# Differential attention: scores on two 64-row halves of the array in three products, and one joint maximum for each softmax component

## The chip, the core and the metric

The program runs on one core of a Trainium2 chip. Five engines work side by side, each through its own queue in order: TensorE (PE in the profile, its weight loads PEld), VectorE (DVE), ScalarE (ACT), GpSimd (POOL), and SyncE (SP), which here only issues transfers. The metric is the device time of one execution in microseconds (us), less is better; a time of before is the median of three runs.

## The reference

Two layers; each normalises x (2048 rows of 1024), projects it, feeds three head groups, joins them through an output projection and adds the result to x. The change touches the middle group alone, differential attention with 4 heads, each with two score components of 64 dimensions:

```python
q = rope(q, pos) * (DIFF_HD ** -0.5)      # (2, B, 4 heads, L, 64)
k = rope(k, pos)
def block(qblk):                          # 128 queries
    s = jnp.einsum('cbhqd,cbhkd->cbhqk', qblk, k).astype(jnp.float32)
    p = jax.nn.softmax(s, axis=-1)
    w = p[0] - lam * p[1]
    return jnp.einsum('bhqk,bhkv->bhqv', w.astype(v.dtype), v)
o = lax.map(block, qb)
o = rms_norm(o, norm_w) * (1.0 - lambda_init)
```

The other two groups are gated linear recurrences; the part of them that reads their carried states (`Inter` below) is computed in the same stage of the kernel as the attention.

## The kernel before, in words

Each layer runs through a projection stage (with the scans of the recurrences), the attention stage, and the output projection. In the attention stage a `Unit` is 128 queries of one head, so a layer has 64 units and the program 128. Products keep fp32 accuracy by a split in a high and a low part: q is split in `aqh` and `aql` (by POOL, L723 and L725, for 256 queries at once), k in its two parts when it is made. The 128 partitions of `ks` hold the 64 dimensions of k's high part and the 64 of its low part, those of q hold the 64 dimensions twice; one 128-row matmul of `aqh` with `ks` therefore gives two products, that of `aql` two more (L866, L867).

A unit passes through four *steps*, one for each score tile of 128 queries by 1024 keys: steps 0 and 1 are the first and second half of the keys for component 0, steps 2 and 3 those for component 1. PE's step is: `scores` (four matmuls of 512 columns into a score tile `s` of two banks), `values` (`po`, the weights times v, for an earlier unit), `transposes` (`pt`, of an earlier unit's weights). DVE takes each tile's maximum (`mx`, L871); ACT takes the exponentials (`e`, L880) out of the tile, and with that frees it; DVE forms e0 + factor * e1 (`combine`, L909); PE transposes that, ACT copies the transposed weights to SBUF (`wt`, L919), PE multiplies them with v.

For component 0 both exponentials wait for the maximum over both tiles (L874, then `exps` in step 2). For component 1 each tile is taken with its own maximum as soon as that is there (step 3 for the tile of step 2, step 0 of the next unit for the tile of step 3); `lows`, `weights`, `total` and `factors` bring the two halves to one scale afterwards.

The order within every engine's queue is written by hand: `tc.manual_schedule` keeps the order of the `at_lag` calls, where lag is the number of steps after the unit's first one. Score tiles come from `two_banks`: three buffers in rotation, so that a tile is written when the third tile before it has been read. `Inter`, one for every second unit from unit 16 to 46 (16 in a layer), takes one turn of this rotation as well: its 12 matmuls `poi` (L816) are issued ahead of the scores of step 3, and ACT's `fetch` (L821) frees it in the step after.

```python
def two_banks(name):
    turn[0] += 1
    key, bufs = (("b", 2), ("b", 2), ("t", 1))[turn[0] % 3]
    return psum[key][1].tile([P, 2, 512], F32, tag="two", name=name, bufs=bufs)
```

The transposed tiles `pt` have one buffer beside that of `po`. POOL has q's split, the multiplication of the result by the gate, the state updates at the stage's start (L768, L771), Inter's sums, and the split of the output weights near the stage's end (`load_wo`, units 50 to 57).

Of the kernel before, what the change touches and what calls it, by code (L numbers as in the profile page):

```python
# [16 lines left out]
ALU = mybir.AluOpType  # L17
# [43 lines left out]
def tile_hybrid_encoder(  # L61
# [178 lines left out]
    for l in range(DEPTH):  # L240
# [15 lines left out]
        with ExitStack() as s1:  # L256
# [67 lines left out]
            def do_qk(c0, cb, which, part):  # L324
                hc = slice(4 * cb, 4 * cb + 4)
                w = wload(c0 + 256 * cb, 256, part, halves=True)
                for g in (2 * part, 2 * part + 1):
# [5 lines left out]
                    for half, (a, b, op) in enumerate(((p1, p2, ALU.subtract), (p2, p1, ALU.add))):  # L333
# [382 lines left out]
            def load_q(h, qp):  # L716
                qr = ak.tile([P, 2, 256], F32, tag="aq", name="aq", bufs=2)
                for half in range(2):
                    for s in range(2):
                        p0 = 64 * half + 32 * s  # L720
# [27 lines left out]
        with ExitStack() as s2:  # L748
# [93 lines left out]
            class Unit:  # L842
                """One block of 128 queries of one head; s counts its tiles of scores (component, half of the keys)."""

                def __init__(self, i):
# [8 lines left out]
                    self.sm = at.tile([P, 4], F32, tag="sm", name="sm", bufs=4)  # L854
                    self.gm = at.tile([P, 10], F32, tag="gam", name="gam", bufs=4)
# [13 lines left out]
                def maxima(self, k):  # L869
                    mx = self.mx  # L870
                    nc.vector.tensor_reduce(mx[:, k:k + 1], self.s[k].rearrange("p a n -> p (a n)"), axis=AX.X, op=ALU.max,  # L871
                                            negate=True)
# [10 lines left out]
                def lows(self):  # L883
                    nc.vector.tensor_tensor(self.mx[:, 5:6], self.mx[:, 2:3], self.mx[:, 3:4], op=ALU.min)

                def sums(self):
                    gm, sm = self.gm, self.sm
                    nc.vector.tensor_tensor(gm[:, 2:3], sm[:, 0:1], sm[:, 1:2], op=ALU.add)

                def sums2(self):  # L890
                    gm = self.gm
                    nc.vector.tensor_scalar(gm[:, 1:2], gm[:, 2:3], neglam, None, op0=ALU.mult)
# [228 lines left out]
```

## Time and profile before

| | us |
|---|---|
| runs | 3752.49, 3755.73, 3758.89; median 3755.73 |
| span of the profiled execution, first to last instruction | 3752.0 |
| mean granted TensorE clock over the span | 0.982 of full speed |
| busy: PE | 3534.9 (94%) |
| busy: DVE | 2691.2 (72%) |
| busy: ACT | 2203.1 (59%) |
| busy: POOL | 1868.5 (50%) |

The profile has no time of the profiled execution other than its span; the median lies 3.7 us above it. Busy shares are means over stages: the score matmuls run from 1034.1 to 1670.0 us in the first layer and from 2902.4 to 3538.3 us in the second, together 34% of the span. A matmul's end is modelled (its record lasts longer than the time until the next one starts), so PE's pace is read from starts.

### The profile page before, as it was taken

How to read it: one execution, taken by the hardware profiler on the slowest of the kernel's cores; microseconds unless marked ns; L12 is line 12 of the kernel's file. 1: busy time of each engine (PE TensorE's matmuls, PEld its weight loads, DVE VectorE, ACT ScalarE, POOL GpSimd, SP SyncE). 2: the span in 40 equal slices, each digit the busy share in tenths (PEclk: the TensorE clock that was granted, in tenths of full speed). 3: DMA queues.
4: the chain of work that ended last, by engine and by line, in shares of the span. 5: the costliest groups of instructions: out<-in, count | busy, mean ns of one | idle time of the engine just before them, and what ended most of it. 6: DMA issues, size and time to landing. Idle time of an engine off the chain costs nothing.

```text
span 3752.0 us, 62823 instructions
## 1 busy us (share of the span) xinstructions
PE 3534.9 (94%) x22976; PEld 3175.5 (85%) x22976; DVE 2691.2 (72%) x4122; ACT 2203.1 (59%) x5140; POOL 1868.5 (50%) x1854
## 2 busy tenths in 40 slices
PE   8999989988989999899999999999889899998999
PEld 7898978877978999788888989889779789997887
DVE  5422789988499999985324238898784999999733
ACT  4521577755568888774225125776555778887722
POOL 3545655565576666520035455555555756664200
PEclk9999999999999999999999999999999999999999
DMA  4443444444441332214334444444444413322133
GB/s 156 133 136 128 134 129 138 137 123 135 131 136 33 117 119 85 66 32 133 120 115 150 125 127 136 129 137 140 126 126 132 126 39 117 115 79 66 38 134 114
DMA packets 293652, 430.54 MB, mean 115 GB/s; under 512 B 42400, under 2 KB 185312, under 8 KB 291040
## 3 DMA queue, kind: packets, MB, share of 16 engines
q1 hardware_dynamic: 268896, 333.71, 28.7%
q0 software_dynamic: 22336, 90.71, 8.3%
q8 instruction: 182, 2.98, 0.3%
q10 hardware_dynamic: 2112, 2.10, 0.2%
q14 instruction: 126, 1.03, 0.1%
HBM read 275.82 MB, written 152.57 MB: 114 GB/s over the span
## 4 chain that ended last, share of the span: by engine, by line
PE 51%; DVE 27%; DMA 10%; issue 4%; POOL 4%; ACT 3%; SPq 1%; DVEq 0%; POOLq 0%; ACTq 0%
PE pp L306 11%; PE pob L1031 9%; PE po L926 8%; PE pp L297 6%; DVE mx L871 5%; PE s L866 4%; PE s L867 4%; PE pt L915 4%; DMA wraw<-in_w_in_dram 3%; DVE e L909 3%; DVE qt L612 3%; DVE pr L545 3%; DVE att L605 2%; DMA cs<-c_rope 2%; PE poi L816 1%
## 5 line engine op out<-in xcount | busy, mean ns | idle before, releaser
L880 ACT ACTIVATE e<-s,mx 128x1024 f32<-128x1024 f32 x512 | 570.5, 1118 | 146.6 <-DVE mx L871 107.3
L871 DVE TENSOR_REDUCE mx<-s 128x1 f32<-128x1024 f32 x512 | 621.3, 1215 | 36.7 <-PE s L867 35.9
L306 PE MATMUL pp<-wlo,hhi 128*128 128x256 f32 (+1 forms) x2048 | 591.0, 289 | 7.8 <-POOL wlo L224 7.7
L926 PEld LDWEIGHTS po<-vt,wt 128*128 128x128 f32 x4096 | 533.2, 191 | 70.0 <-ACT o L933 30.0
L306 PE MATMUL pp<-whi,hlo 128*128 128x256 f32 (+1 forms) x2048 | 591.8, 289 | 0.1
L306 PE MATMUL pp<-whi,hhi 128*128 128x256 f32 (+1 forms) x2048 | 588.0, 287 | 3.0 <-DVE whi L223 3.0
L926 PE MATMUL po<-vt,wt 128*128 128x128 f32 x4096 | 544.1, 276 | 17.4 <-ACT o L933 17.4
L866 PE MATMUL s<-ks,aqh 128*128 128x512 f32 x1024 | 449.7, 439 | 28.0 <-ACT e L880 26.5
L297 PE MATMUL pp<-hhi,whi 128*128 128x512 f32 x1024 | 412.1, 402 | 3.7 <-DVE zg L428 2.4
L297 PE MATMUL pp<-hhi,wlo 128*128 128x512 f32 x1024 | 410.1, 400 | 0.0
L297 PE MATMUL pp<-hlo,whi 128*128 128x512 f32 x1024 | 410.0, 400 | 0.0
L867 PE MATMUL s<-ks,aql 128*128 128x512 f32 x1024 | 404.0, 395 | 5.2 <-POOL aql L725 5.2
L306 PEld LDWEIGHTS pp<-wlo,hhi 128*128 128x128 f32 x2048 | 393.1, 192 | 8.8 <-POOL wlo L224 8.8
L306 PEld LDWEIGHTS pp<-whi,hhi 128*128 128x128 f32 x2048 | 395.0, 193 | 4.1 <-DVE whi L223 3.8
L306 PEld LDWEIGHTS pp<-whi,hlo 128*128 128x128 f32 x2048 | 393.8, 192 | 0.7 <-DVE hlo L195 0.3
L909 DVE SCALAR_TENSOR_TENSOR e<-e,gam 128x1024 f32<-128x1024 f32 x256 | 367.1, 1434 | 4.5
L919 ACT COPY wt<-pt 128x512 f32<-128x512 f32 x512 | 300.5, 587 | 100.1 <-PE pt L915 98.3
L915 PE MATMUL pt<-ident,e 128*128 128x128 f32 x2048 | 310.5, 274 | 14.5 <-DVE e L909 8.7
L610 POOL TENSOR_TENSOR kt<-kt,nt 128x512 f32<-128x512 f32 x144 | 191.7, 1334 | 206.0 <-DVE kl L588 106.7
L915 PEld LDWEIGHTS pt<-ident,e 128*128 128x128 f32 x2048 | 238.7, 141 | 23.3 <-ACT wt L919 11.3
L866 PEld LDWEIGHTS s<-ks,aqh 128*128 128x128 f32 x1024 | 194.4, 190 | 61.3 <-ACT e L880 36.5
L214 POOL DMA_DIRECT2D wraw<-in_w_in_dram x124 | 97.4, 786 | 283.0 <-DVE sso L1038 183.8
(198 smaller groups left out, 8165.7 us busy)
## 6 DMA issues: line engine op xcount, KB each, us to landing
wraw<-in_w_in_dram POOLq DMA_DIRECT2D x116, 512.0 KB, 4.8
cs<-c_rope SPq DMA_DIRECT2D x32, 512.0 KB
dr_gate<-z SPq DMA_DIRECT2D x64, 256.0 KB
aq<-dr_q SPq DMA_DIRECT2D x256, 64.0 KB
ks<-dr_k POOLq DMA_DIRECT2D x16, 1024.0 KB, 8.1
y<-dr_y SPq DMA_DIRECT2D x32, 512.0 KB
dr_qs<-qt SPq DMA_DIRECT2D x48, 256.0 KB
qs<-dr_qs SPq DMA_DIRECT2D x24, 512.0 KB
```

The lines of the kernel that those rows point to most:

```text
L297: nc.tensor.matmul(ps.rearrange("p (a t) -> p a t", t=P), w[a][:, k, c:c + P], b[g][:, :, k], start=n == 0, stop=n == 3 * KC - 1)
L306: nc.tensor.matmul(ps, b[g][:, t % 4, k], w[a][:, k, :n], start=cnt == 0, stop=cnt == 3 * KC - 1)
L610: nc.gpsimd.tensor_tensor(ka, ka, custom(tt, toff + 1, [(tn - 1, 2), (2, n2), (0, h)]), op=ALU.mult)
L866: nc.tensor.matmul(s[:, i], self.qh[:, c, js], kk, start=True, stop=False)
L867: nc.tensor.matmul(s[:, i], self.ql[:, c, js], kk, start=False, stop=True)
L871: nc.vector.tensor_reduce(mx[:, k:k + 1], self.s[k].rearrange("p a n -> p (a n)"), axis=AX.X, op=ALU.max, negate=True)
L880: nc.scalar.activation(self.es[c][:, n * 1024:(n + 1) * 1024], self.s[kk].rearrange("p a n -> p (a n)"), AF.Exp, bias=self.mx[:, m:m + 1], ...
L909: nc.vector.scalar_tensor_tensor(es[0][:, hs], es[1][:, hs], gm[:, 8 + n:9 + n], es[0][:, hs], op0=ALU.mult, op1=ALU.add)
L915: nc.tensor.transpose(pt[:, i], self.es[0][:, (4 * q + i) * P:(4 * q + i + 1) * P], ident)
L919: nc.scalar.copy(wt, self.pt[q])
L926: nc.tensor.matmul(self.po, self.wt[q][:, i], self.v[:, k], start=k == 0, stop=k == NT - 1)
L1031: nc.tensor.matmul(pos[:, n], a[:, k], b[k][:, n * 512:(n + 1) * 512], start=cnt == 0, stop=cnt == 3 * KC - 1)
```

## The change

k is stored and loaded otherwise: rows 0 to 63 of `ks` hold the 64 dimensions of k for one half of every 1024 keys, rows 64 to 127 for the other half, and the high and the low part lie behind one another in the free dimension. The two products for a 512-key half of a score tile run on 64 rows of the array, the other half's on the other 64 rows. Three products are formed in place of four (low times low is left out), so a step has six 64-row matmuls where it had four 128-row ones. Each head's `ks` comes in eight transfers in place of two. Component 1 is treated like component 0: both exponentials wait for the joint maximum of both tiles, in step 0 of the next unit. `lows`, `weights`, `total`, `factors` go; `sums` adds two columns at once, `factor` takes the place of `factors`, `combine` has one factor for both halves.

```diff
-                            nc.sync.dma_start(dr_k[hc, half, 0, :, sl], rh.bitcast(F32))
-                            nc.sync.dma_start(dr_k[hc, half, 1, :, sl], u)
+                            nc.sync.dma_start(dr_k[hc, 0, half, :, sl], rh.bitcast(F32))
+                            nc.sync.dma_start(dr_k[hc, 1, half, :, sl], u)
...
-                    k = ak.tile([P, L], F32R, tag="ks", name="ks", bufs=4)
-                    nc.gpsimd.dma_start(k, dr_k[2 * h + c].rearrange("a s p t -> (a s p) t"))
+                    k = ak.tile([P, 2, 2, 512], F32R, tag="ks", name="ks", bufs=4)
+                    for r in range(2):
+                        for s in range(2):
+                            nc.gpsimd.dma_start(k[64 * r:64 * r + 64, s],
+                                                dr_k[2 * h + c, s].rearrange("a p (n r t) -> r (a p) n t", r=2, t=512)[r])
...
-                    for i in range(2):
-                        kk = self.ks[c][:, (2 * n + i) * 512:(2 * n + i + 1) * 512]
-                        nc.tensor.matmul(s[:, i], self.qh[:, c, js], kk, start=True, stop=False)
-                        nc.tensor.matmul(s[:, i], self.ql[:, c, js], kk, start=False, stop=True)
+                    for i, (q, part) in enumerate(((self.qh, 0), (self.qh, 1), (self.ql, 0))):
+                        for r in range(2):
+                            rows = slice(64 * r, 64 * r + 64)
+                            nc.tensor.matmul(s[:, r], q[rows, c, js], self.ks[c][rows, part, n], start=i == 0, stop=i == 2)
...
-                    if k == 1:
-                        nc.vector.tensor_tensor(mx[:, 4:5], mx[:, 0:1], mx[:, 1:2], op=ALU.min)
-
-                def exps(self, k):
-                    for kk in ((), (0, 1), (2,), (3,))[k]:
-                        c, n = divmod(kk, 2)
-                        m = 4 if c == 0 else kk
-                        nc.scalar.activation(self.es[c][:, n * 1024:(n + 1) * 1024], self.s[kk].rearrange("p a n -> p (a n)"),
-                                             AF.Exp, bias=self.mx[:, m:m + 1], accum_out=self.sm[:, kk:kk + 1])
...
+                    nc.vector.tensor_tensor(mx[:, 4 + c:5 + c], mx[:, 2 * c:2 * c + 1], mx[:, 2 * c + 1:2 * c + 2], op=ALU.min)
+
+                def exps(self, c):
+                    for n in range(2):
+                        nc.scalar.activation(self.es[c][:, n * 1024:(n + 1) * 1024],
+                                             self.s[2 * c + n].rearrange("p a n -> p (a n)"), AF.Exp,
+                                             bias=self.mx[:, 4 + c:5 + c], accum_out=self.sm[:, n, c:c + 1])
...
-                    nc.vector.tensor_scalar(gm[:, 1:2], gm[:, 2:3], neglam, None, op0=ALU.mult)
-                    nc.vector.tensor_scalar(gm[:, 3:4], gm[:, 2:3], EPS, gm[:, 2:3], op0=ALU.mult, op1=ALU.mult)
...
-                    nc.vector.tensor_scalar(gm[:, 8:10], gm[:, 4:6], gm[:, 0:1], gm[:, 1:2], op0=ALU.mult, op1=ALU.mult)
...
+                    nc.vector.scalar_tensor_tensor(gm[:, 4:5], gm[:, 0:1], neglam, gm[:, 2:3], op0=ALU.mult, op1=ALU.mult)
...
-                def weights(self):
-                    nc.scalar.activation(self.gm[:, 4:6], self.mx[:, 2:4], AF.Exp, scale=-1.0, bias=self.mx[:, 5:6])
...
-                    at_lag(1, "exps")
-                    at_lag(4, "weights", 0)
+                    at_lag(1, "exps", 1, 0)
+                    at_lag(1, "exps", 3, 1)
```

On PE, these rows stand around one `poi` of the kernel before: the score tile of step 3 (`s_14560`), values and transposes, and the next unit's first score tile (`s_14597`).

```order
L816 MATMUL poi_14553<-ust_11063,qs_13705 128x128 x2
L816 MATMUL poi_14553<-ust_11063,qs_13706 128x64 x2
L816 MATMUL poi_14553<-ust_11063,qs_13707 128x64 x2
L866 MATMUL s_14560<-ks_11467,aqh_14343 128x512
L867 MATMUL s_14560<-ks_11467,aql_14345 128x512
L866 MATMUL s_14560<-ks_11467,aqh_14343 128x512
L867 MATMUL s_14560<-ks_11467,aql_14345 128x512
L926 MATMUL po_14506<-vt_11469,wt_14546 128x128 x4
L915 MATMUL pt_14569<-ident_64,e_14352 128x128 x4
L866 MATMUL s_14597<-ks_11465,aqh_14343 128x512
L867 MATMUL s_14597<-ks_11465,aql_14345 128x512
```

At such a place of the changed kernel PE has, with the tile of step 2 (`s_15211`) shown too:

```order
L870 MATMUL s_15211<-ks_13363,aqh_15018 128x512 x4
L870 MATMUL s_15211<-ks_13363,aql_15020 128x512 x2
L919 MATMUL po_15189<-vt_13368,wt_15202 128x128 x4
L908 MATMUL pt_15222<-ident_64,e_14903 128x128 x4
L819 MATMUL poi_15239<-ust_11069,qs_14862 128x128 x2
L819 MATMUL poi_15239<-ust_11069,qs_14863 128x64 x2
L819 MATMUL poi_15239<-ust_11069,qs_14864 128x64 x2
L870 MATMUL s_15246<-ks_13363,aqh_15018 128x512 x4
L870 MATMUL s_15246<-ks_13363,aql_15020 128x512 x2
L919 MATMUL po_15189<-vt_13368,wt_15232 128x128 x4
L908 MATMUL pt_15257<-ident_64,e_15027 128x128 x4
L870 MATMUL s_15282<-ks_13358,aqh_15018 128x512 x4
```

The order of the groups is the same; a score tile is six matmuls (four with `aqh`, two with `aql`). The first tile of the next unit, `s_15282`, takes the buffer of the tile of step 2, `s_15211`, the third before it.

On ACT, before, around the `fetch` of that `poi` (`sq`); `s_14530` is the tile of step 2 and `pt_14569` the transposes that PE has just ahead of the next unit's first tile:

```order
L880 ACTIVATE e_14476,sm_14350<-s_14501,mx_14349 128x1024
L919 COPY wt_14578<-pt_14539 128x512
L880 ACTIVATE e_14477,sm_14350<-s_14530,mx_14349 128x1024
L919 COPY wt_14614<-pt_14569 128x512
L821 COPY sq_14616<-poi_14553 128x512
L880 ACTIVATE e_14477,sm_14350<-s_14560,mx_14349 128x1024
L929 ACTIVATE gam_14351<-mx_14349 128x2
```

On ACT, in the changed kernel:

```order
L882 ACTIVATE e_15156,sm_15025<-s_15182,mx_15024 128x1024
L912 COPY wt_15264<-pt_15222 128x512
L912 COPY wt_15300<-pt_15257 128x512
L824 COPY sq_15302<-poi_15239 128x512
L882 ACTIVATE e_15157,sm_15025<-s_15211,mx_15024 128x1024
L882 ACTIVATE e_15157,sm_15025<-s_15246,mx_15024 128x1024
```

The exponential of the tile of step 2 has moved from ahead of the copy of these transposes to behind it and behind the fetch.

On DVE, one unit's rows before, from the second half of `combine` to the reduction of the tile of step 3 (`mx<-s` are the four reductions):

```order
L909 SCALAR_TENSOR_TENSOR e<-e,gam 128x1024
L871 TENSOR_REDUCE mx<-s 128x1
L897 SCALAR_TENSOR_TENSOR gam<-gam,sm 128x2
L871 TENSOR_REDUCE mx<-s 128x1
L874 TENSOR_TENSOR mx<-mx 128x1
L901 RECIPROCAL gam<-gam 128x1
L905 TENSOR_SCALAR gam<-gam 128x2
L909 SCALAR_TENSOR_TENSOR e<-e,gam 128x1024
L871 TENSOR_REDUCE mx<-s 128x1
L888 TENSOR_TENSOR gam<-sm 128x1
L871 TENSOR_REDUCE mx<-s 128x1
L892 TENSOR_SCALAR gam<-gam,neglam 128x1
```

And in the changed kernel:

```order
L902 SCALAR_TENSOR_TENSOR e<-e,gam 128x1024
L873 TENSOR_REDUCE mx<-s 128x1 x2
L878 TENSOR_TENSOR mx<-mx 128x1
L887 TENSOR_TENSOR gam<-sm 128x2
L890 RECIPROCAL gam<-gam 128x1
L873 TENSOR_REDUCE mx<-s 128x1
L898 SCALAR_TENSOR_TENSOR gam<-gam,neglam 128x1
L894 TENSOR_SCALAR gam<-gam 128x1
L902 SCALAR_TENSOR_TENSOR e<-e,gam 128x1024
L873 TENSOR_REDUCE mx<-s 128x1
L878 TENSOR_TENSOR mx<-mx 128x1
```

L892, L897 and L905 are gone, L898 (`factor`) is new, and the first half of `combine` stands behind the reduction of the tile of step 2, where it stood ahead of it.

## Rows read from the trace of the kernel before

**Rows 1.** Windows of the first attention stage; the columns are in the first line.

```profile
core 0: us, PE busy (x) PEld busy (x) DVE busy (x) ACT busy (x) POOL busy (x), PEclk, DMA share, GB/s
...
1040.00:1140.00 100.00, 87.20 (x546) 74.75 (x547) 96.06 (x140) 70.49 (x155) 79.73 (x71) 0.97 0.44 119
...
1240.00:1340.00 100.00, 99.88 (x716) 92.17 (x715) 95.00 (x154) 83.64 (x197) 61.62 (x84) 1.00 0.38 117
...
1540.00:1640.00 100.00, 89.03 (x605) 77.93 (x603) 98.29 (x145) 73.78 (x174) 42.22 (x41) 1.00 0.17 57
```

**Rows 2.** Chain that ended last, 1240 to 1300 us: start, us, what.

```profile
by line: PE po L926 34.2%; PE s L866 19.5%; PE s L867 18.0%; PE pt L915 16.7%; PE poi L816 7.1%; ACT e L880 2.0%; DVE mx L871 1.9%; DVE mx L874 0.8%; issue 0.2%
...
1250.17 0.89 PE po L926 x8
1251.06 0.44 PE pt L915 x4
1252.43 0.89 PE po L926 x8
```

**Rows 3.** Timeline around one poi: start us, us, engine, line, tile, shape.

```profile
1301.59 1.52 PE L816 MATMUL poi<-ust,qs 128*128 128x128 f32 x12
...
1304.82 0.60 PE L915 MATMUL pt<-ident,e 128*128 128x128 f32 x4
...
1305.20 0.49 PE L866 MATMUL s<-ks,aqh 128*128 128x512 f32 x1
...
1305.51 0.59 ACT L919 COPY wt<-pt 128x512 f32<-128x512 f32 x1 [0.37 <-PE pt L915]
...
1305.53 0.39 PE L867 MATMUL s<-ks,aql 128*128 128x512 f32 x1
...
1305.76 0.39 PE L866 MATMUL s<-ks,aqh 128*128 128x512 f32 x1
...
1305.99 0.59 ACT L821 COPY sq<-poi 128x512 f32<-128x512 f32 x1
...
1306.47 1.13 ACT L880 ACTIVATE e<-s,mx 128x1024 f32<-128x1024 f32 x1
```

**Rows 4.** Timeline where a score tile waits for an exponential.

```profile
1569.66 1.11 ACT L880 ACTIVATE e<-s,mx 128x1024 f32<-128x1024 f32 x1 [0.90 <-DVE mx L874]
...
1570.92 0.50 PE L866 MATMUL s<-ks,aqh 128*128 128x512 f32 x1 [0.52 <-ACT e L880]
...
1571.26 0.39 PE L867 MATMUL s<-ks,aql 128*128 128x512 f32 x1
```

**Rows 5.** Timeline of PE where matmuls with 32 columns end (128*32).

```profile
75.37 0.93 PE L414 MATMUL ppa<-ident,low 128*32 128x128 f32 x7
76.05 0.48 PE L297 MATMUL pp<-hhi,whi 128*128 128x512 f32 x1
76.37 0.39 PE L297 MATMUL pp<-hlo,whi 128*128 128x512 f32 x1
```

**Rows 6.** DVE's groups, 1240 to 1440 us: count, busy us, mean ns, idle before.

```profile
L871 DVE TENSOR_REDUCE mx<-s 128x1 f32<-128x1024 f32 x82 | 99.7, 1216 | 7.7 <-PE s L867 7.3
L909 DVE SCALAR_TENSOR_TENSOR e<-e,gam 128x1024 f32<-128x1024 f32 x41 | 53.6, 1307 | 0.7
L905 DVE TENSOR_SCALAR gam<-gam 128x2 f32<-128x2 f32 x21 | 15.1, 719 | 0.8
...
L888 DVE TENSOR_TENSOR gam<-sm 128x1 f32<-128x1 f32 x20 | 9.6, 482 | 0.0
...
L892 DVE TENSOR_SCALAR gam<-gam,neglam 128x1 f32<-128x1 f32 x20 | 4.0, 201 | 0.0
...
L897 DVE SCALAR_TENSOR_TENSOR gam<-gam,sm 128x2 f32<-128x2 f32 x20 | 3.0, 150 | 0.0
```

**Rows 7.** Two gaps on PE's timeline, and the windows behind them (columns of Rows 1).

```profile
828.07 1.12 PE L630 MATMUL pd<-ident,pr 128*128 128x128 f32 x4 [2.84 <-ACT att L603]
...
828.20:831.60 3.40, 3.40 (x11) 2.84 (x12) 3.40 (x5) 1.44 (x4) 2.63 (x3) 0.52 0.66 218
...
2693.26 0.66 PE L630 MATMUL pd<-ident,pr 128*128 128x128 f32 x4 [2.85 <-ACT att L603]
...
2693.40:2696.80 3.40, 3.40 (x18) 2.82 (x18) 3.40 (x5) 1.43 (x4) 2.64 (x3) 1.00 0.70 197
```

**Rows 8.** POOL's groups, 1240 to 1440 us: the issue of a head's keys.

```profile
L710 POOL DMA_DIRECT2D ks<-dr_k x2 | 1.2, 582 | 0.0
```

More of the change, by code (lines that the diff above doesn't have):

```diff
@@ L718, in load_q @@
                 for half in range(2):
-                    for s in range(2):
-                        p0 = 64 * half + 32 * s
+                    for r in range(2):
+                        p0 = 64 * r + 32 * half
                         nc.sync.dma_start(qr[p0:p0 + 32], dr_q[2 * h:2 * h + 2, half, :, qp * 256:(qp + 1) * 256].rearrange("c p t -> p c t"))
@@ L853, in __init__ @@
                     self.mx = at.tile([P, 6], F32, tag="mx", name="mx", bufs=4)
-                    self.sm = at.tile([P, 4], F32, tag="sm", name="sm", bufs=4)
-                    self.gm = at.tile([P, 10], F32, tag="gam", name="gam", bufs=4)
+                    self.sm = at.tile([P, 2, 2], F32, tag="sm", name="sm", bufs=4)
+                    self.gm = at.tile([P, 5], F32, tag="gam", name="gam", bufs=4)
                     self.s, self.pt, self.wt = [None] * 4, [None] * 4, [None] * 4
@@ L863, in scores @@
                     js = slice(self.j * P, (self.j + 1) * P)
-                    for i in range(2):
-                        kk = self.ks[c][:, (2 * n + i) * 512:(2 * n + i + 1) * 512]
-                        nc.tensor.matmul(s[:, i], self.qh[:, c, js], kk, start=True, stop=False)
-                        nc.tensor.matmul(s[:, i], self.ql[:, c, js], kk, start=False, stop=True)
+                    for i, (q, part) in enumerate(((self.qh, 0), (self.qh, 1), (self.ql, 0))):
+                        for r in range(2):
+                            rows = slice(64 * r, 64 * r + 64)
+                            nc.tensor.matmul(s[:, r], q[rows, c, js], self.ks[c][rows, part, n], start=i == 0, stop=i == 2)
@@ L869, in maxima, with joint @@
                 def maxima(self, k):
+                    nc.vector.tensor_reduce(self.mx[:, k:k + 1], self.s[k].rearrange("p a n -> p (a n)"), axis=AX.X, op=ALU.max,
+                                            negate=True)
+                def joint(self, c):
                     mx = self.mx
-                    nc.vector.tensor_reduce(mx[:, k:k + 1], self.s[k].rearrange("p a n -> p (a n)"), axis=AX.X, op=ALU.max,
-                                            negate=True)
-                    if k == 1:
-                        nc.vector.tensor_tensor(mx[:, 4:5], mx[:, 0:1], mx[:, 1:2], op=ALU.min)
@@ L886, in sums @@
+                def exps(self, c):
[3 more added lines that the diff above has]
+                                             bias=self.mx[:, 4 + c:5 + c], accum_out=self.sm[:, n, c:c + 1])
                 def sums(self):
-                    gm, sm = self.gm, self.sm
-                    nc.vector.tensor_tensor(gm[:, 2:3], sm[:, 0:1], sm[:, 1:2], op=ALU.add)
@@ L890, in sums2, with inverse, floor @@
-                def sums2(self):
+                    nc.vector.tensor_tensor(self.gm[:, 0:2], self.sm[:, 0], self.sm[:, 1], op=ALU.add)
+                def inverse(self):
+                    nc.vector.reciprocal(self.gm[:, 2:3], self.gm[:, 1:2])
+                def floor(self):
                     gm = self.gm
-                    nc.vector.tensor_scalar(gm[:, 1:2], gm[:, 2:3], neglam, None, op0=ALU.mult)
-                    nc.vector.tensor_scalar(gm[:, 3:4], gm[:, 2:3], EPS, gm[:, 2:3], op0=ALU.mult, op1=ALU.mult)
@@ L895, in total @@
[L895 to L903 removed]
+                    nc.vector.tensor_scalar(gm[:, 3:4], gm[:, 0:1], EPS, gm[:, 0:1], op0=ALU.mult, op1=ALU.mult)
@@ L904, in factors, with factor @@
+                def factor(self):
                     gm = self.gm
-                    nc.vector.tensor_scalar(gm[:, 8:10], gm[:, 4:6], gm[:, 0:1], gm[:, 1:2], op0=ALU.mult, op1=ALU.mult)
+                    nc.vector.scalar_tensor_tensor(gm[:, 4:5], gm[:, 0:1], neglam, gm[:, 2:3], op0=ALU.mult, op1=ALU.mult)
                 def combine(self, n):
-                    es, gm, hs = self.es, self.gm, slice(n * 1024, (n + 1) * 1024)
-                    nc.vector.scalar_tensor_tensor(es[0][:, hs], es[1][:, hs], gm[:, 8 + n:9 + n], es[0][:, hs],
+                    es, hs = self.es, slice(n * 1024, (n + 1) * 1024)
+                    nc.vector.scalar_tensor_tensor(es[0][:, hs], es[1][:, hs], self.gm[:, 4:5], es[0][:, hs],
@@ L975, in tile_hybrid_encoder @@
                     at_lag(7, "transposes")
-                    at_lag(4, "lows", 0)
-                    at_lag(6, "combine", 0, 0)
-                    at_lag(6, "combine", 2, 1)
-                    at_lag(5, "total", 0)
-                    at_lag(3, "sums", 0)
-                    at_lag(0, "maxima")
-                    at_lag(5, "inverse", 0)
-                    at_lag(3, "sums2", 0)
-                    at_lag(5, "factors", 0)
+                    at_lag(6, "inverse", 0)
+                    at_lag(6, "combine", 2, 1)
+                    at_lag(0, "maxima")
+                    at_lag(0, "joint", 1, 0)
+                    at_lag(0, "joint", 3, 1)
+                    at_lag(5, "sums", 0)
+                    at_lag(6, "factor", 0)
+                    at_lag(6, "floor", 0)
+                    at_lag(6, "combine", 0, 0)
                     at_lag(8, "copy")
                     inter(1, "fetch")
-                    at_lag(1, "exps")
-                    at_lag(4, "weights", 0)
+                    at_lag(1, "exps", 1, 0)
+                    at_lag(1, "exps", 3, 1)
                     at_lag(10, "norm", 3)
```

9 lines of the change are left out of this document (removed).

## The prediction, made before the changed kernel ran

> **What bounds the kernel now.** I read the windows of the attention stage first, because the change touches nothing else: over 1240 to 1340 us PE is busy 99.88 of 100 us, DVE 95.00, ACT 83.64 and POOL 61.62; near the stage's start (1040 to 1140) and end (1540 to 1640) PE falls to 87.20 and 89.03 while DVE stays at 96.06 and 98.29 [rows 1]. A busy share of PE is modelled, so I looked next at the chain of waits: between 1240 and 1300 us its PE lines add up to 95.5% [rows 2]. So PE bounds the middle of the stage, DVE its two ends. The second layer repeats this.
>
> A step of PE is read from starts. From one `po` to the next in the chain it is 2.26 us, of which `po` takes 0.89 and `pt` 0.44 [rows 2]; 0.93 are left for the scores, four matmuls of 0.23 (1305.53 to 1305.76) [rows 3]. A unit has four steps, 9.0 us; a unit with an Inter has the 12 `poi` besides. Of a layer's 64 units 16 have an Inter; the two windows where DVE bounds hold about 20 units (200 us at 10 to 11 us); 28 are left, bound by PE and without Inter.
>
> **The scores, six half matmuls for four whole ones.** The trace has no 64-row matmul, so the price is bounded. If the two of a pair run side by side from the start, a step needs 3 x 0.23 = 0.69 us; if one runs after the other, 6 x 0.23 = 1.38. Each matmul has a weight load before it, and `po` and `pt`, which do little else than load weights, run at 0.89 / 8 = 0.11 us each [rows 2]. I take it that the second of a pair starts one load later than the first and that the loads of the next pair (0.22) hide behind 0.23: 0.11 + 0.69 = 0.80. That is a gain of 0.13 a step, 0.5 a unit (bounds: gain 0.96, loss 1.8).
>
> The half matmuls stand between whole ones, so the array changes its division twice a step. Nearest to that are seven matmuls with 32 columns: they take 0.93 us, which is 6 x 0.11 + 0.27, as four transposes of the whole array take 0.60 = 3 x 0.11 + 0.27 [rows 3, 5]; and the second 128-column matmul behind them follows the first after 0.32 us (76.05 to 76.37), where after transposes without any change it takes 0.33 (1305.20 to 1305.53). I price the switch at nothing. The Trainium skill speaks against that: its page "TensorEngine Tiling (Array Packing)", section "Key Properties", says that a change of the tiling mode drains TensorE. It gives no time; the trace disagrees for columns, and no run here shows rows. By the row the sum stays as below, by the rule it would be that of the last but one rival.
>
> **The exponentials of component 1, moved.** This edit costs. The tile of step 2 was read by ACT in step 3. Now its exponential stands in ACT's queue behind the copy of the transposes that PE makes at the end of step 3. In a unit without Inter the next tile to use that buffer is that of step 1 of the next unit, a step later, which leaves room. In a unit with an Inter, `poi` takes a turn of the three buffers, and the tile that needs the buffer is the next unit's *first*, directly behind those transposes on PE. There ACT's chain lies open: transposes, copy, fetch, exponential, then the score tile. Each link has a row: `pt` starts at 1304.82, the copy at 1305.51, fetch at 1305.99, the exponential at 1306.47 and lasts 1.13, to 1307.60 [rows 3]; a score tile that waits for an exponential starts 0.15 after its end (1569.66 + 1.11 = 1570.77, start 1570.92) [rows 4]: 1307.75. Without the wait the scores start at 1305.20 [rows 3]. PE stands for 2.55 us, since everything else in its queue (`values`, the next transposes) is behind that tile. It does not depend on how fast the half matmuls are. 32 such units: **+82 us**.
>
> The stall may also lower PE's clock. After a gap of 2.84 us the granted clock was 0.52 in the next 3.4 us, that is mostly the lower level of 1.2 GHz, and 11 matmuls were recorded there; after one of 2.85 us it stayed at 1.00, with 18 [rows 7]. Half of the stalls, at 7/18 of 3.4 = 1.3 us: 32 x 0.65 = **+21** (bounds 0 and 42).
>
> **What is won.** In the 32 Inter units PE stays on the path, so the scores' gain comes in full: 32 x 0.5 = **-15** (bounds -31 and +58).
> In the 56 others that PE bounds it comes only in part. The tile of step 2 must now pass reduction, `factor` (priced as L897), `floor` (as L892), half of `combine`, the reduction of step 3, the joint minimum and an exponential before its buffer is free three steps later: 1.22 + 0.15 + 0.20 + 1.31 + 1.22 + 0.15 + 1.13 = 5.4 us [rows 3, 6], with the scores' 0.80 and a hand-over of 0.15 at each change of engine about 6.6, less some overlap at DVE, against 3 x 2.13 = 6.4 us. There is nothing to spare when DVE is late, and it is late often: the small operations L905 and L888 take 719 and 482 ns on the mean [rows 6], while L897, with more operands, takes 150. I take half: 56 x 0.25 = **-14** (bounds 0 and -54).
> In about 40 units that DVE bounds, DVE loses L905, L892 and L897 and gets `factor`: 0.72 + 0.20 + 0.15 - 0.15 = 0.92 us a unit [rows 6]. L905's mean is mostly waiting, and part of that will fall to its neighbours: 40 x 0.5 = **-20** (bounds 0 and -37).
>
> Priced at nothing: ACT's `weights`, one small operation a unit less on an engine with 16% idle [rows 1]; the stores of k (as many, as large); six more issues for each head's keys at 0.58 us each [rows 8], 3.5 us on POOL, which is idle 38% of the time [rows 1], and a head's keys are asked for twelve units ahead (without that cover: 8 heads x 3.5 = 28 us).
>
> Sum on the profiled execution: 3752 + 82 + 21 - 15 - 14 - 20 = 3806; the median lies 3.7 us above the span: **3810 us**.
>
> **Rivals.**
> *Side by side from the start* (0.69 a step): the Inter units gain 0.96 each, 31; the others, held by the chain through DVE, about 0.5, 28; with 82 + 21 - 31 - 28 - 20 = +24 the time is 3780. For it: nothing in the trace forbids loads ahead of a matmul of the other half; against it: each load in the trace of before starts at a matmul's start. The Trainium skill's "TensorE: Matmul & The Clock Gate", section "The mechanism", has it this way: matmuls on different row groups run together, some 4 ns apart; no run here shows it. 14%.
> *The gains outrun the stall*, the other side: side by side, and no chain through DVE, so that 56 units gain 0.96 (-54) and 40 gain 0.92 (-37), and the clock stays: 82 - 31 - 54 - 37 = -40, 3716. It decides once the mean unit of 128 gains more than 0.64 us. Against it: DVE has only 5% to spare now [rows 1]. 14%.
> *The halves run one after the other*: a unit of PE is 1.8 longer. 88 x 1.8 = 158, and about 0.6 in the 40 units that DVE bounds, 24: 82 + 21 + 158 + 24 = +285, 4041. For it: no row shows two matmuls at once. 5%.
> *The switch drains the array*: a lone matmul's 0.27 less its 0.11, twice a step, 1.28 a unit over 88 units: +113 on the sum, 3923. 6%.
> *The stall does not come* (ACT is early enough) and the rest nets to little, within 0.2% of before, 7.5 us, about what a measurement of this kernel tells from no change: 6%.
>
> **How the numbers follow.** The forecast has 55%; with its own bounds (clock 0 to 42, the two partial gains from nothing to full) it reaches from 3770 to 3865. The range takes in side by side, no change and the nearer part of the gains, and leaves out the serial halves, the drain and the far gain: 3745 to 3870. Slower 0.55 + 0.14 + 0.05 + 0.06 = 0.80, faster 0.14, same 0.06; 0.03 of the forecast's share I move to its near side, where the gains come in fuller than taken: slower 0.77, same 0.07, faster 0.16.
>
> **What would show it.** In the profile after: `s` waiting for ACT's `e`, some 2.5 us, 16 times a layer, always the first tile behind the transposes after a `poi`; in these units PE busy falls, DVE's share too. Starts of half matmuls 0.11 apart in a pair and 0.23 from pair to pair; the six and the next `po` within 0.80. If pairs start together, or 0.23 apart, the rivals hold. PEclk below 1.00 in the middle of the stage shows the clock's part. I am wrong if the first tile after a `poi` does not wait, or if units without Inter fall below 8.4 us.

## The result, and the profile after

| | before | after |
|---|---|---|
| median, us | 3754.11 (3752.49 to 3758.89) | 3894.95 (3889.14 to 3902.55) |
| span of the profiled execution, us | 3752.0 | 3894.6 |
| mean granted clock | 0.982 | 0.972 |

The medians are of four runs each. The change made the kernel slower: ratio 1.0371, 95% interval 1.0357 to 1.0386, 141 us. The sign was forecast, the size (3810, range to 3870) was not.

The busy line of the page, and windows (columns of [rows 1]) of the first stage, of the second, and of 3.4 us behind one stall in each:

```profile
PE 3620.2 (93%) x24000; PEld 3072.1 (79%) x24000; DVE 2551.1 (66%) x3738; ACT 2174.9 (56%) x5012; POOL 1851.3 (48%) x1902
...
1040.00:1140.00 100.00, 79.92 (x528) 57.88 (x529) 77.22 (x99) 59.58 (x127) 80.43 (x73) 0.86 0.52 120
...
1240.00:1340.00 100.00, 90.70 (x665) 71.01 (x665) 69.41 (x104) 67.92 (x156) 52.23 (x76) 0.97 0.43 104
...
1540.00:1640.00 100.00, 92.77 (x670) 71.06 (x671) 76.93 (x108) 69.07 (x157) 43.82 (x56) 0.97 0.18 57
...
3195.00:3295.00 100.00, 93.91 (x711) 73.32 (x710) 73.05 (x109) 72.70 (x167) 56.25 (x83) 1.00 0.42 105
...
1297.00:1300.40 3.40, 3.40 (x16) 2.69 (x17) 1.22 (x1) 0.93 (x3) 2.93 (x7) 0.52 0.39 111
...
3267.00:3270.40 3.40, 3.40 (x25) 2.41 (x26) 1.26 (x2) 3.23 (x8) 3.17 (x4) 1.00 0.00 0
```

Against [rows 1], DVE has fallen from 95 to 69 of 100 us in the middle of the stage and from 98 to 77 at its end: it bounds little there any more. PE has lost 9 us of 100 in the middle as well. The layers differ: the first has the lower clock. And the stage's start (1040 to 1140) is worse than before, PE 80 against 87, at a granted clock of 0.86 against 0.97.

The chain around one `poi` of the first layer (start, us, what):

```profile
1290.80 1.29 PE poi L819 x12
1292.09 0.89 PE s L870 x6
1292.98 1.09 PE po L919 x8
1294.07 0.45 PE pt L908 x4
...
1294.60 0.59 ACT wt L912
1295.18 0.49 ACT sq L824
1295.67 1.12 ACT e L882 x2
...
1296.83 1.42 PE s L870 x6
1298.25 2.00 PE po L919 x8
1300.25 0.64 PE pt L908 x4
```

This is the stall that was forecast, link by link: transposes, copy, fetch, exponential, first score tile, 2.31 us from the transposes' end (1294.52) to the tile. Then comes a step of 1.42 + 2.00 + 0.64 = 4.06 us: that is the window above at a granted clock of 0.52, mostly the lower level of 1.2 GHz. By the trace's record of the clock, ten of this layer's sixteen stalls are followed by such a fall; behind the other six the clock stays at the upper level. An undisturbed step is the one ahead of it: 0.89 + 1.09 + 0.44 = 2.42 us, where before it had 2.26 [rows 2], although the scores stream for a shorter time.

The same place in the second layer:

```profile
3265.28 0.45 PE pt L908 x4
...
3265.81 0.59 ACT wt L912
3266.39 0.50 ACT sq L824
...
3266.93 0.97 PE s L870 x6
3267.90 1.09 PE po L919 x8
3268.99 0.44 PE pt L908 x4
```

Here the tile waits only for the fetch, 1.20 us, and the clock stays at 1.00, behind all sixteen stalls. The order on the engines is the same; the buffer is not. In this layer the rotation gives the next unit's first tile the buffer of the `poi`, which the fetch frees, and not the one of the tile of step 2.

One step near the stage's start, on PE and its weight loads; the first row is of a window that holds one pair alone. The last two rows are of the kernel before, the load of a tile's last score matmul and those of `po`:

```profile
1091.89 0.49 PE L870 MATMUL s<-ks,aqh 64*128 64x512 f32 x2
...
1091.89 0.30 PEld L870 LDWEIGHTS s<-ks,aqh 64*128 64x128 f32 x4 [0.17 <-issue]
...
1092.45 0.40 PE L870 MATMUL s<-ks,aql 64*128 64x512 f32 x2
...
1092.78 0.97 PEld L919 LDWEIGHTS po<-vt,wt 128*128 128x128 f32 x8 [0.36 <-issue]
...
1305.76 0.19 PEld L867 LDWEIGHTS s<-ks,aql 128*128 128x128 f32 x1
...
1305.99 1.10 PEld L926 LDWEIGHTS po<-vt,wt 128*128 128x128 f32 x8
```

Both halves of a pair lie within 0.49 us, as long as one whole matmul (1305.20 in [rows 3]), and by the trace they start 3 to 4 ns apart, so they run side by side from the start. The page "TensorE: Matmul & The Clock Gate" of the Trainium skill, section "The mechanism", says so of different row groups; the trace agrees, with these 3 to 4 ns. Three pairs of 0.23 are 0.69 us. But PE's loads stand idle for 0.17 us ahead of the first half and for 0.36 us ahead of `po`, with "issue" as the releaser: nothing that the profile shows is waited for. In the kernel before, `po`'s loads start 0.04 us after the load ahead of them ends. So the engine pauses at each change of the division; that it empties there is how I read the pause. A step without that would be 0.69 + 0.89 + 0.44 = 2.02 us; the 0.40 more are 0.20 for each change.

POOL's groups from 1045 us to the split of q for unit 6, first before, then after, and the PE row that waits for it:

```profile
L771 POOL TENSOR_TENSOR ust<-ust,st 64x512 f32<-64x512 f32 x7 | 10.8, 1544 | 0.4
L768 POOL TENSOR_TENSOR st<-ust,tst 64x512 f32<-64x512 f32 x8 | 9.5, 1184 | 10.6 <-DMA ust<-dr_u 10.3
```

```profile
L774 POOL TENSOR_TENSOR ust<-ust,st 64x512 f32<-64x512 f32 x11 | 16.0, 1456 | 0.7
L771 POOL TENSOR_TENSOR st<-ust,tst 64x512 f32<-64x512 f32 x12 | 14.5, 1210 | 14.0 <-DMA ust<-dr_u 13.4
L712 POOL DMA_DIRECT2D ks<-dr_k x8 | 4.7, 601 | 0.0
```

```profile
1104.28 1.22 PE L870 MATMUL s<-ks,aqh 64*128 64x512 f32 x4 [7.49 <-POOL aqh L726]
```

Eight state updates more stand ahead of the split (23 against 15, 30.5 us against 20.3), which the diff doesn't touch: POOL's place for them is the scheduler's. With the keys' eight issues (4.7 us, against 1.2 for two in [rows 8]) PE waits 7.5 us there, and another 2.5 us for the low part; the second layer repeats it.

### The profile page after: what moved, and what is told of

It is laid out like the page before. It is cut to its first block, busy times and chain, and to the rows that moved or that the text cites. A ratio compares the mean times of both kernels' runs of the same rounds, so it can differ in the third digit from the quotient of the medians.

```text
span 3894.6 us, 64423 instructions
## 1 busy us (share of the span) xinstructions
PE 3620.2 (93%) x24000; PEld 3072.1 (79%) x24000; DVE 2551.1 (66%) x3738; ACT 2174.9 (56%) x5012; POOL 1851.3 (48%) x1902
## 4 chain that ended last, share of the span: by engine, by line
PE 59%; DVE 16%; DMA 10%; POOL 6%; issue 5%; ACT 4%; SPq 1%; DVEq 0%; POOLq 0%; ACTq 0%
PE po L919 13%; PE pp L306 11%; PE s L870 10%; PE pob L1021 9%; PE pp L297 6%; PE pt L908 5%; DMA wraw<-in_w_in_dram 3%; DVE qt L612 2%; DVE att L605 2%; DVE pr L545 2%; DMA cs<-c_rope 2%; DMA ust<-dr_u 1%; PE poi L819 1%; ACT e L882 1%; POOL ru L338 1%
## 5 line engine op out<-in xcount | busy, mean ns | idle before, releaser
L919 PEld LDWEIGHTS po<-vt,wt 128*128 128x128 f32 x4096 | 505.5, 194 | 195.2 <-issue 138.9
L919 PE MATMUL po<-vt,wt 128*128 128x128 f32 x4096 | 602.5, 291 | 9.3 <-ACT o L923 9.1
L870 PE MATMUL s<-ks,aqh 64*128 64x512 f32 x2048 | 383.9, 453 | 90.6 <-ACT e L882 55.0
L902 DVE SCALAR_TENSOR_TENSOR e<-e,gam 128x1024 f32<-128x1024 f32 x256 | 346.7, 1355 | 0.0
L870 PEld LDWEIGHTS s<-ks,aqh 64*128 64x128 f32 x2048 | 157.7, 190 | 181.0 <-issue 68.1
L297 PEld LDWEIGHTS pp<-hhi,whi 128*128 128x128 f32 x1024 | 196.7, 192 | 46.2 <-DVE zg L428 2.8
```

The source lines that it names most:

```text
L297: nc.tensor.matmul(ps.rearrange("p (a t) -> p a t", t=P), w[a][:, k, c:c + P], b[g][:, :, k], start=n == 0, stop=n == 3 * KC - 1)
L870: nc.tensor.matmul(s[:, r], q[rows, c, js], self.ks[c][rows, part, n], start=i == 0, stop=i == 2)
L902: nc.vector.scalar_tensor_tensor(es[0][:, hs], es[1][:, hs], self.gm[:, 4:5], es[0][:, hs], op0=ALU.mult, op1=ALU.add)
L919: nc.tensor.matmul(self.po, self.wt[q][:, i], self.v[:, k], start=k == 0, stop=k == NT - 1)
```

## The experiments

The ratio of each is against the kernel before on its own chip; intervals are 95%. Differences between two runs are of their medians, some of them from different chips, where the kernel before took between 3754 and 3759 us. Where units are counted, a unit lasts from the start of its first score matmul to that of the next unit's, in the profiled execution.

**rows_only.** The kernel before with k's layout, its loads and the six half matmuls of the change; the softmax as before.

> The kernel before with the scores alone changed: k's layout, its eight loads a head, six 64-row matmuls a tile; the two softmax components stay as they were. Theory (the array drains at each change between 64-row and whole matmuls, about 0.2 us each, twice a step, against 0.24 us that the shorter streaming saves): a step of PE is 2.42 us as in the changed kernel, a unit 9.67 us, a unit with an Inter 11.1, no wait of a first tile behind a poi; 88 units x 0.64 = +56 us, and up to 15 more at the two starts of the stage if the eight loads delay POOL: 3810 to 3825. Rival (the half matmuls are as fast as the profile of single pairs says, and the longer step comes from the moved exponentials): step at or below 2.26, time 3754 or less.

3822.99 us, ratio 1.0182 (1.0167 to 1.0197), 67 us. The chain shows the steps of the changed kernel (0.89, 1.09, 0.44) and no stall. The theory holds; the rival, that the longer step comes from the moved exponentials, falls. In units 16 to 47, where a unit without Inter now takes 9.67 us in place of 9.04, the two layers lose 33 us.

**joint_only.** The changed kernel with k and `scores` of before:

```diff
-                    for i, (q, part) in enumerate(((self.qh, 0), (self.qh, 1), (self.ql, 0))):
...
+                    for i in range(2):
+                        kk = self.ks[c][:, (2 * n + i) * 512:(2 * n + i + 1) * 512]
```

> The kernel before with the joint maximum and its new order alone: four whole matmuls a tile, k as before in two loads a head. Theory (drain and stall are separate costs): units without Inter stay at 9.03 us; the first tile behind a poi waits for 2.3 to 2.6 us in the first layer and 1.2 to 1.4 in the second, where the buffer it gets is that of the poi: 16 x 2.5 + 16 x 1.4 = 62, plus 10 to 20 for the clock in the first layer, less about 20 where DVE bounded: 3805 to 3820. Rival (the moved exponentials also lengthen the units without Inter): 9.6 us there too, 3870 or more.

3849.32 us, ratio 1.025 (1.0233 to 1.0267), 94 us: more than expected. Ahead of the first `poi` units without Inter keep their pace (2.27 us from `po` to `po` in the chain, 1198.71 to 1200.98), and the stall comes. The clock was sized too low: the window 1240 to 1340 us has 0.92, lower than the changed kernel's 0.97 (fifteen of the layer's sixteen stalls are followed by a fall, where the changed kernel had ten), and in the second layer (3195 to 3295) 1.00:

```profile
1240.00:1340.00 100.00, 90.70 (x591) 82.40 (x591) 67.22 (x98) 66.09 (x154) 49.57 (x77) 0.92 0.33 101
...
3195.00:3295.00 100.00, 95.13 (x676) 86.41 (x675) 77.81 (x117) 77.72 (x181) 51.93 (x79) 1.00 0.28 82
```

**four_switches.** `scores` issues the first pair of a tile, and the other two stand behind `values` (`products` holds the loop of before, over some of the pairs):

```diff
-                        for r in range(2):
...
+                    self.products(k, 0, 1)
...
+                def rest(self, k):
+                    self.products(k, 1, 3)
...
                     at_lag(9, "values")
+                    at_lag(0, "rest")
```

> The changed kernel with the last two pairs of each tile's half matmuls moved behind `values`, so that the array changes its division four times a step in place of two; the same instructions otherwise. Theory (each change drains): another 0.3 to 0.4 us a step, about 100 units x 4 x 0.35 = +140, near 4035. Rival (the changes are free and the half matmuls are slow by themselves): 3895 as the changed kernel, within 10 us.

4123.57 us, ratio 1.0986 (1.0968 to 1.1004), 229 us above the changed kernel. One step of its chain in the second layer:

```profile
3337.49 0.43 PE s L877 x2
3337.91 1.09 PE po L929 x8
3339.00 0.66 PE s L877 x4
3339.67 0.59 PE pt L918 x4
```

2.77 us with the same matmuls that take 2.42 with two changes and would take 2.02 with none: 0.75 for four changes, 0.19 each, and in each of the four rows (0.23, 0.89, 0.46 and 0.44 without). So the price goes with the number of changes, and not with that of half matmuls. The total exceeds the forecast of +140, which counted 100 units; over all 128 the 0.35 a step make 179 us. The other 50 us were not taken apart; that ACT's chain gets longer too, as the rest of a tile comes later and with it its maximum and exponential, is argued and not shown.

**phase2.** The changed kernel with the rotation set alike in both layers:

```diff
             units, inters = {}, {}
+            turn[0] = 2
```

> The changed kernel with the counter of the score buffers set at the start of both attention stages, so that in both layers the first tile behind a poi gets the poi's own buffer, as only the second layer had it. Theory (the stall is 2.32 us where that tile waits for an exponential and 1.22 where it waits for the poi's fetch, and the clock falls only behind the longer one): layer 0 takes on the 12.24 and 9.67 us of layer 1, 16 x 1.11 + 11 x 1.57 = 35 us less: 3860. Rival (the low clock of the first layer has another cause than the longer stall): only 16 x 1.11 = 18 less, 3877. If the buffers don't matter: 3895.

3860.58 us, ratio 1.0282 (1.0267 to 1.0298): 34 us less than the change, as expected. The same window of the first layer has a clock of 1.00 now:

```profile
1240.00:1340.00 100.00, 93.91 (x708) 72.77 (x708) 73.21 (x109) 72.73 (x168) 56.59 (x84) 1.00 0.42 106
```

**fetch_early.** phase2 with the fetch ahead of the copy:

```diff
+                    inter(1, "fetch")
                     at_lag(8, "copy")
-                    inter(1, "fetch")
```

> The kernel of phase2 with ACT's fetch of the poi moved ahead of the copy of the transposed weights in the same step. Theory (what is left of the stall, 1.22 us, is the first tile waiting for the fetch, which stands behind a copy that waits for PE's transposes): the fetch runs as soon as the poi is there, the wait goes, a unit with an Inter is 9.67 + 1.28 = 10.95 us as in rows_only, 32 x 1.29 = 41 us less than phase2: 3820. Rival (the wait moves on, to the tile of step 1, whose buffer is that of an exponential of component 1): 12.2 us stay, 3860.

3819.74 us, ratio 1.0165 (1.0146 to 1.0184), 41 us less than phase2. No first tile behind a `poi` waits any more: stall and clock together were 75 us (80 with each run set against its own kernel before), and two lines take them away with the joint maximum in place.

**grouped.** fetch_early with `values`, `transposes`, `scores` in every second step, so that two tiles stand together.

> The kernel of fetch_early with PE's order turned round in every second step (values, transposes, scores), so that two score tiles stand next to each other and the array changes its division twice in two steps in place of four times. Theory (0.2 to 0.22 us a change): 0.4 to 0.45 us less in two steps, a unit 8.8 to 8.9 us in place of 9.67, about 90 units x 0.8 = 72 less: 3748, and less gained where DVE (about 8.5 us of work a unit) holds it. Rival (the half matmuls, not the changes, are what costs): 3820. Third: two tiles at once come too early for their buffers, so PE waits for exponentials and part of the gain goes: 3780 to 3800.

4193.51 us, ratio 1.1167 (1.1143 to 1.1192), the opposite of what I expected. What PE waits for from 1340 to 1540 us (sum, times, longest):

```profile
PE po L919 <- ACT o L923: 28.2, 15, 2.0
PE pt L908 <- DVE e L902: 9.3, 7, 1.3
```

With `values` and `transposes` moved up, the first product of a unit stands before the copy of the last one's result, which ACT makes behind two exponentials. The run tells nothing of the changes of division.

**pairs.** fetch_early with the scores moved instead: both tiles of a component in every second step, their exponentials a step earlier, `factor` and the first `combine` ahead of the reduction.

```diff
-                    at_lag(0, "scores")
+                    if f % 2 == 0:
+                        at_lag(0, "scores")
+                        if f < 4 * NU:
+                            units[f // 4].scores(f % 4 + 1)
...
-                    at_lag(1, "exps", 1, 0)
-                    at_lag(1, "exps", 3, 1)
+                    at_lag(0, "exps", 1, 0)
+                    at_lag(0, "exps", 3, 1)
```

> The kernel of fetch_early with the scores of two tiles issued together in every second step, without moving values and transposes; the exponentials run in the step of their joint maximum, and factor and the first combine stand ahead of the reductions. Theory (0.2 us a change, half of the changes gone, and nothing held back this time): a unit 8.8 to 8.9 us in place of 9.67, 70 us less: 3750. Rival (as in grouped, another engine's order holds PE): units above 9.3, 3790 or more. DVE has about 8.5 us of work in a unit, so less than 8.8 is not to be had.

3793.03 us, ratio 1.0097 (1.008 to 1.0114): 27 us gained of the 70 expected. Two steps of its chain:

```profile
1173.78 1.58 PE s L870 x12
1175.36 1.09 PE po L919 x8
1176.45 0.44 PE pt L908 x4
1176.89 1.13 PE po L919 x8
1178.02 0.44 PE pt L908 x4
```

Twelve half matmuls take 1.58, six 0.89, so one change is saved there and one at `po`; but the second `po` takes 1.13 in place of 0.89, directly behind the transposes, as it waits for ACT. 4.68 us against 2 x 2.42 = 4.84. This is ahead of the first Inter. In units 16 to 47 little of it is left: a unit without Inter takes 9.64 us, against 9.67 in fetch_early. By units, 22 us of the gain come in the last sixteen of both layers.

**joint_fetch** and **joint_pairs.** The controls: fetch_early and pairs with four whole matmuls a tile, where no division changes.

> fetch_early with the scores as in the kernel before: four whole matmuls, k in two loads. It holds the joint maximum without the stall and without any change of the array's division. Theory (stall, clock and drain were all that cost): units 9.03 to 9.2 us, with an Inter 10.3 to 10.45, 3750 to 3760, as the kernel before; rival (the joint maximum costs by itself): 3780 or more.

> pairs with four whole matmuls a tile: the same order on every engine, but no change of division to save. Theory (grouping gains by the changes alone): two tiles take 1.87 us in place of 1.59, the waits of pairs stay (0.2 to 0.3 us in two steps), a unit about 9.5 us, slower than joint_fetch by 0.3 to 0.5 a unit: 3790 to 3800. Rival (the new order itself gained): 27 us faster than joint_fetch, about 3730.

joint_fetch 3771.9 us, ratio 1.0038 (1.0025 to 1.0051), 15 us above the kernel before and 12 above the forecast. So stall, clock and drain were not all: the joint maximum costs something by itself, as the rival had it, though less than the rival's 3780. PE's weight loads wait for this from 1240 to 1440 us (sum, times, longest):

```profile
PEld po L916 <- ACT o L920: 8.7, 20, 0.5
```

A unit's first `po` waits 0.43 us for the copy of the last unit's result, which ACT now makes behind two exponentials in place of one; a unit without Inter takes 9.49 us in place of 9.04. With half matmuls this is hidden: a unit without Inter takes 9.67 us with the joint maximum (fetch_early) and without it (rows_only).

joint_pairs 3776.97, ratio 1.0055 (1.0035 to 1.0074). Grouping does not gain without the half matmuls: its four rows behind the scores are

```profile
1193.47 0.89 PE po L916 x8
1194.36 0.44 PE pt L905 x4
1194.80 1.13 PE po L916 x8
1195.93 0.44 PE pt L905 x4
```

with the same 0.24 too much in the second `po`, and nothing to save. In the two steps shown, the half matmuls of pairs save 0.40 and pay these 0.24: 0.16, the 4.84 - 4.68 above. In the last sixteen units of both layers joint_pairs gains 14 us on joint_fetch without any change of division to save, in units 16 to 47 it loses 9; so the total moves by 5 us only, less than I expected, and most of what pairs gained is the new order's.

**late_keys** and **grouped_late.** The keys and values of the next head are asked for at unit 10 in place of unit 4 (`f % 64 == 40`), in fetch_early and in grouped.

> The kernel of fetch_early with the next head's keys and values asked for at unit 10 in place of unit 4, when POOL's state updates are done. Theory (the eight issues, 4.75 us in a row on POOL, delay the split of q that unit 6 waits for): units 5 and 6 come down from 19.9 and 16.0 us to about 13 each, 9 us a layer, 18 less than fetch_early: 3801. Rival (the scheduler's order of state updates ahead of the split of q is what delays it, not the issues): within 5 us of fetch_early.

> grouped and late_keys together. If both costs are separate the differences add up: 3748 - 18 = 3730, faster than the kernel before by 0.6%. If the units at the stage's start are bound by DVE and POOL anyway, the sum falls short and the time is near that of grouped.

3824.86 us, ratio 1.0177 (1.016 to 1.0195), no better than fetch_early, and 4198.76 (1.1184, 1.116 to 1.1207), as grouped was already held elsewhere. The rival holds: with the eight issues gone, the scheduler puts more state updates in their place, and PE waits for the split of q as long as before (7.8 and 2.7 us).

**state_spread.** fetch_early with the state updates in the hand-written order:

```diff
+                    if 10 <= f < 52 and (f - 10) % 3 < 2:
+                        state((f - 10) // 3 * 2 + (f - 10) % 3)
```

> The kernel of fetch_early with the 28 state updates on POOL put into the hand-written order, two in three steps from step 10 on, in place of where the scheduler sets them. Theory (POOL's queue at the stage's start is what units 1 to 7 wait for: the scheduler puts more state updates ahead of the split of q than it did in the kernel before): units 5 and 6 come down from 19.9 and 15.9 us to 12 or 13 each, and the first sixteen units together from about 176 us to about 165: 10 to 12 us a layer, 3820 - 22 = 3798. Rival (the units wait for the transfers of q or of the keys): within 5 us of fetch_early.

3797.69 us, ratio 1.0106 (1.0091 to 1.0121), 22 less than fetch_early. What PE waits for from POOL between 1034 and 1134 us:

```profile
PE s L870 <- POOL aqh L726: 1.6, 1, 1.6
PE s L870 <- POOL aql L728: 1.5, 1, 1.5
```

3.1 us in place of 11.3 in fetch_early (8.6 and 2.7) and 10 in the changed kernel.

**before_state** and **rows_state** are the same edit on the kernel before and on rows_only:

> The kernel before with the state updates alone put into the hand-written order, to see what that edit is worth without the change. Its units 5 and 6 take 12.2 and 13.3 us where 10.5 would be DVE's pace: at best 4 us a layer, 3748; no change if DVE bounds those units anyway, 3755.

> rows_only with the state updates in the hand-written order. Theory (of rows_only's 67 us, some 45 are the drain and some 22 POOL's queue at the two starts of the stage): 3801, units 5 and 6 at 11 to 14 us. Rival (its start is held by the loads of the keys): 3820.

3769.7 us, ratio 1.003 (1.0021 to 1.004): 11 us more than the kernel before: there the scheduler's own order was the better one, which I had not expected. rows_state 3809.58, ratio 1.0141 (1.0118 to 1.0165): 15 of rows_only's 67 us went with POOL's new order, and not 22; 52 are left to the half matmuls.

**pairs_state** and **pairs_norm.** pairs with the state updates of state_spread, and then with ACT's `norm` a step later (`at_lag(11, "norm", 3)`, the store at 12).

> pairs and state_spread together: if the two costs are separate, 3750 - 22 = 3728, 0.7% faster than the kernel before.

> pairs_state with ACT's norm of a finished unit moved one step later, behind a copy of the transposes, and the store behind it. If ACT's queue holds PE in pairs (transposes that wait 0.2 us for the copy): 0.2 to 0.3 us a unit less, 3768 - 25 = 3743, faster than the kernel before. If DVE's chain (reductions, joint, factor, combine) holds it: 3765 to 3770 as pairs_state.

3768.59 us, ratio 1.0026 (1.0015 to 1.0037): the gain of the two edits adds up, from a worse pairs than expected. 3753.61, ratio 0.9991 (0.9979 to 1.0004): 15 us of the 25 expected. In units 16 to 47 one without Inter falls from 9.64 to 9.14 us, so ACT's queue did hold pairs there. This is the best version with half matmuls, and not to be told from the kernel before. Its order was not run with whole matmuls, so what the half matmuls add in it is not shown.

## Why the prediction was wrong, step by step

**The switch** is the step that failed: "I price the switch at nothing." I inferred it from matmuls with 32 *columns* [rows 5]; the change divides *rows*. Two changes cost 0.40 us a step. That a matmul leaves part of the array unused is not what costs, as four of 96 rows in the kernel before show, which stand between whole ones at 0.23 us from start to start:

```profile
98.21 0.39 PE L297 MATMUL pp<-hhi,wlo 128*128 128x512 f32 x1
98.44 1.09 PE L426 MATMUL ppz<-a,wa 96*128 96x512 f32 x4
99.36 0.40 PE L297 MATMUL pp<-hhi,whi 128*128 128x512 f32 x1
```

Whether those of 32 columns divide the array at all is not shown, so the row could not carry the inference. The rival that had it right also had its mechanism: its price, a lone matmul's 0.16 twice a step, 0.32, is near the 0.40 that was measured, but I gave it 6%. The Trainium skill says in "TensorEngine Tiling (Array Packing)", section "Key Properties", that a change of the tiling mode drains the array; every run with half matmuls agrees, at about 0.2 us a change. I had let a trace of columns speak against it. The scores themselves were better than forecast: 0.69 a step (the rival "side by side"), not 0.80. The two rivals were true at once, and I had set them against each other. By the step: -0.24 + 0.40 = +0.16 in place of -0.13; by the runs: +52 us (rows_state) in place of -29.

**The stall** was right in place, links and engine. Its size, "32 such units: +82", assumed that a tile always waits for the third tile before it; that holds in the first layer (2.31 us, not 2.55), but in the second the first tile gets the `poi`'s buffer and waits for the fetch, and 1.20 are left: 16 x 2.31 + 16 x 1.20 = 56 us. The clock was +21 in the forecast; it fell behind ten of the thirty-two stalls, all in the first layer, at 1.64 us each, 16 us. By the runs both together are 75 to 80 us (phase2 and fetch_early) in place of 103; joint_only and joint_fetch, the same pair with whole matmuls, differ by 77.

**"Priced at nothing"** for POOL's six more issues failed as well: cover was averaged over the middle of the stage (38% idle [rows 1]), while the first of a layer's three loads (at units 4, 20 and 36) falls into its start, where POOL was 80% busy in the same rows. The price came by a way that I had not thought of, the scheduler's reordering: 22 us (state_spread). I had looked at the order of PE, ACT and DVE and not of POOL. It comes with the scores' edit: between 1034 and 1134 us PE waits for POOL 10.6 us in rows_only, and in joint_only, which has whole matmuls and two loads a head, no such wait is listed. Whether the six issues or the half matmuls move the scheduler is not shown; late_keys shows that the issues' place is not what holds PE.

**DVE's units**: state_spread lies 39 us above the kernel before, rows_state 52; so under the half matmuls the joint maximum with its stall removed gives back about 14 where I had 20, by units 11 of it in the first sixteen of both layers and 5 in the last sixteen. Without them it gives nothing back: joint_fetch lies 15 us above the kernel before, by the copy behind two exponentials, which the prediction does not have.

Against the forecast's 3810 the scores make +81, POOL +22, stall and clock -28, DVE +6: 81 of the 85 us that it was too low; the rest is below what sums over runs on different chips can tell. These terms hold in this order of the edits alone. With the joint maximum first, it costs 15 us and the half matmuls 24 more (joint_fetch, state_spread), and the edit of POOL's order is worth -22, -15 and +11 us in fetch_early, rows_only and the kernel before.

The lower end of the forecast's own reach, 3770, does not follow from its bounds: clock at 0, and both partial gains in full (54 and 37), give 3732. The result lies beyond the other end, so nothing hangs on it.

## What to carry to other kernels

Matmuls on two halves of the rows are priced with the two changes of division around them (0.2 us each here); their own saving (0.24 a tile) was smaller than these 0.40. Two tiles together save 0.48, but no run here made a net gain of that. When a queue is relieved, look for what was hidden behind it: the joint maximum's own cost shows only in the control without half matmuls. A stall behind an extra user of a rotation depends on which buffer the rotation hands out, so look at the waits of every stage in the built program, not of one. When an edit adds to a queue that a scheduler fills, read that queue's new order around the busiest stretch, even where the diff doesn't touch it.

## What the runs showed of the hardware

The drain has about the same price in both directions: 0.20 where `po` follows the half matmuls, 0.20 to 0.21 where half matmuls follow whole ones, 0.15 before `pt` (four_switches). Matmuls of 96 rows between whole ones had no such price (0.23 us from start to start). The clock fell after stalls of 2.31 us, behind ten of sixteen in the changed kernel and fifteen of sixteen in joint_only, and never after those of 1.20, in the second layer of either or in both layers of phase2; where it fell, one step cost 4.06 us in place of 2.42, so such a stall of 2.31 us cost another 1.64 behind it. Two halves on the two row groups took 0.49 us together, the time of one whole matmul of 512 columns.
